# Down-projection terms added to x by VectorE instead of by accumulating DMAs, and a second buffer for the fourth block's parts

## The chip, the core and the metric

The kernel runs on one core of a Trainium2 chip. A core has five engines with a queue each, which run their own instructions in order and wait for one another by semaphores: TensorE (PE in the profile, with its weight loads as PEld), VectorE (DVE), ScalarE (ACT), GpSimd (POOL) and SyncE (SP). TensorE multiplies from the on-chip memory SBUF into eight banks of a second memory, PSUM. VectorE and ScalarE read those banks. DMAs move data between the device memory and SBUF and inside SBUF; those that add to what is at the target are issued by GpSimd here. The metric is the device time of one execution in microseconds (us), lower is better.

## The reference

Two layers of an encoder on 512 tokens of width 1024. Each layer is a gated feed-forward block, a mixer and a second feed-forward block; `x` is the residual stream.

```python
def swiglu(h, w1, w3, w2):
    return (jax.nn.silu(h @ w1) * (h @ w3)) @ w2
...
        h = rmsnorm(x, g_ffn1[l])
        x = x + 0.5 * swiglu(h, w1_a[l], w3_a[l], w2_a[l])
...   # the mixer: p = h @ w_in[l], Fourier, convolution and pooling branches, gates, then
        x = x + merged @ w_o[l]
        h = rmsnorm(x, g_ffn2[l])
        x = x + 0.5 * swiglu(h, w1_b[l], w3_b[l], w2_b[l])
```

`w1` and `w3` are 1024 x 2816, `w2` is 2816 x 1024. There are four feed-forward blocks in all. Everything is float32.

## The kernel before

**Layout.** Activations lie with channels on the 128 partitions and the 512 tokens along the row: `x` is eight tiles `x[0]` to `x[7]` of 128 x 512. Each float32 operand of a matmul is cut into a high part and a low part (what the high part's rounding left), and `mm` (L360) makes three matmuls of one product: high by high, high by low, low by high (L362, L363, L364).

**Jobs of seven products.** Most of the work is done in jobs. A job takes two output blocks of 128 channels and two halves of 256 tokens, thus a 2 x 2 block result, and a number of pairs of input blocks (four pairs for products from `x`, whose operand is called n in the profile; three pairs for the down-projections by `w2`, whose operand is called unit). It needs seven block products M1 to M7 instead of eight. `run` (L559) issues them in the order M1, M5, M4 of the job before, M6, M3 of the job before, M2, M7. They share three PSUM banks: M6, M7 and M4 add into the bank in which M1 began, M3 adds into that of M5, and M2 has one of its own. A result is a sum of banks at certain moments: "11" is M1 and M2; "12" is the first bank after M6 and the M5 bank after M3; "22" is the first bank after M7 and M5; "21" is the first bank after M4.

**How a result leaves.** After M1, M6 and M7, `kept` (L572) has ScalarE copy the first bank into a tile `sM1`, `sM6` or `sM7` (L574), so that the next product can add into the bank. `take` (L705) then has VectorE add the other bank to that copy into the tiles `a` or `b`, 256 tokens at a time (through `tt`, L437); "21" is copied to `a` by ScalarE (L715). When `a` or `b` is whole, a down-projection job adds it to `x[m + 1]` or `x[m]` by a DMA of GpSimd (L716, L718).

**Stages.** In each feed-forward block the input blocks of `w2` come in three phases of six. As soon as a phase's operands are there, four down-projection jobs follow one another (for channels 0 and 1, 2 and 3, and so on). That makes twelve such stages in the program. Between them stand jobs that make gate and up products. The rest of `w2` (input blocks 18 to 21) is done by plain products.

**Weights.** A job's weights are four blocks: the two of the first row come as one load into a raw tile (`first`), the third as z and the fourth as w (`fourth`, w22 in the code). VectorE makes sums and differences of them (L232, L233, L239), ScalarE casts the high parts (L193, L208), and the low parts come in one of two ways: VectorE subtracts (L194), or ScalarE writes the negative (L206) and an accumulating DMA of GpSimd adds the weights from device memory once more (L207). The latter way serves the first row (partl) and the fourth block (part22h and part22l, used by M4 alone). Loads are issued by SyncE (L187).

**What sets the order.** `Layout` (L94) gives each step of each job a due time on a planned clock: the planned time of the product that needs it minus a lead from `AHEAD` (for the fourth block's parts, the step "last", 12 us ahead of M4). `Weights.advance` (L257) goes through the list at each product and makes the steps that are due, in the list's order. A step that finds no free buffer (`BUFS`, L153) stops the list there: what is behind it waits as well. A buffer is given back when the last product that reads it is issued. Tiles of the activations (the units) come from a pool of 51 equal ones (`UNITS`).

Of the kernel before, what the change touches and what calls it, by code (L numbers as in the profile page):

```python
# [13 lines left out]
ALU = mybir.AluOpType  # L14
# [19 lines left out]
UNITS = 51  # L34
# [59 lines left out]
class Layout:  # L94
# [3 lines left out]
             "rest": 8.0, "last": 12.0}  # L98
# [50 lines left out]
class Weights:  # L149
# [3 lines left out]
    BUFS = {"raw": 3, "z": 2, "w22": 2, "part": 6, "part22": 1}  # L153
# [153 lines left out]
def encoder(ctx: ExitStack, tc: tile.TileContext, layout, x_in, w_in, consts_in, gain_in, out):  # L307
# [128 lines left out]
    def tt(out, a, b, op=ALU.mult):  # L436
        nc.vector.tensor_tensor(out=out, in0=a, in1=b, op=op)  # L437
# [92 lines left out]

    def multiply(job, q, ps, start):
        hi, lo = weights.product(job, q)
        k, n = job[2]
        ops = state["g"] if job[0][0][:2] == "w2" else state["n"]
        for j in range(n):
            while k // 2 + j not in ops and ops is not state["n"]:
                one()
            b = ops[k // 2 + j]
            mm(ps, cut((hi, lo), j * P, (j + 1) * P), b[q], start and j == 0, j == n - 1, not start)
# [19 lines left out]
    def run(jobs, take, before=(), after=(), between=None):  # L559
# [12 lines left out]
        def kept(b, q, ps):  # L572
            b["s" + q] = tmp.tile([P, Q], F32, tag="s" + q, name="s" + q, bufs=2)
            nc.scalar.copy(b["s" + q], ps)  # L574

        def product(job, b, q):
# [4 lines left out]
            if q in ("M1", "M6", "M7"):  # L581
                kept(b, q, ps)
# [3 lines left out]
            if q == "M2":  # L586
                late.append(lambda: take(job, "11", ps, b["sM1"], late))
            if q == "M7":
                late.append(lambda: take(job, "22", b["M5"], b["sM7"], late))
            if q == "M4":  # L590
                late.append(lambda: take(job, "21", ps, None, late))
            if q == "M3":
                late.append(lambda: take(job, "12", ps, b["sM6"], late))
# [86 lines left out]
    def ffn(l, s, after, first=False, last=False):  # L680
# [24 lines left out]
        def take(job, which, ps, addend, late):  # L705
            c = slice(0, Q) if which[1] == "1" else slice(Q, S)
# [5 lines left out]
            if job[0][0] == "w2" + s:  # L712
                m = job[0][2] // P
                if which == "21":
                    nc.scalar.copy(a[:, c], ps)  # L715
                    late.append(lambda: nc.gpsimd.dma_start(x[m + 1], a, accum_op=ALU.add))  # L716
                elif which == "12":
                    late.append(lambda: nc.gpsimd.dma_start(x[m], b, accum_op=ALU.add))  # L718
                    if m == KD - 2:
                        state["done"] += 1  # L720
                        made(None)
                return
# [480 lines left out]
```

## Time and profile before

| what | value |
| --- | --- |
| median of 3 runs | 2120.56 us (2116.67 to 2122.01) |
| the profiled execution, its time | 2117.35 us |
| its span, first to last instruction | 2115.4 us |
| mean granted TensorE clock | 0.982 |
| busy share PE, DVE, ACT, POOL | 96%, 70%, 67%, 25% |
| DMA, mean over the span | 181 GB/s |

How to read what follows. A row of a group has the line, the engine, the operation, the tiles written and read (`out<-in`, buffer numbers left out), shapes and count, then the busy time in us and the mean of one in ns, then the engine's idle time just before these instructions and what ended it. A row of the view of waits has the engine, tile and line that waited, what ended the wait, the total in us, the number of waits and the longest. A timeline row has the start in us from the span's start, the duration in us, engine, line, operation and tiles, and in brackets the idle time before it with its releaser. A line may be that of a helper: L437 is every VectorE operation on two tensors. Matmuls overlap in the pipeline, so one lasts longer than the distance to the next.

### The profile page before, as it was taken

How to read it: one execution, taken by the hardware profiler on the slowest of the kernel's cores; microseconds unless marked ns; L12 is line 12 of the kernel's file. 1: busy time of each engine (PE TensorE's matmuls, PEld its weight loads, DVE VectorE, ACT ScalarE, POOL GpSimd, SP SyncE). 2: the span in 40 equal slices, each digit the busy share in tenths (PEclk: the TensorE clock that was granted, in tenths of full speed). 3: DMA queues.
4: the chain of work that ended last, by engine and by line, in shares of the span. 5: the costliest groups of instructions: out<-in, count | busy, mean ns of one | idle time of the engine just before them, and what ended most of it. 6: DMA issues, size and time to landing. Idle time of an engine off the chain costs nothing.

```text
span 2115.4 us, 38561 instructions
## 1 busy us (share of the span) xinstructions
PE 2023.3 (96%) x14886; PEld 1921.1 (91%) x14886; DVE 1487.8 (70%) x2403; ACT 1418.1 (67%) x2442; POOL 537.8 (25%) x628
## 2 busy tenths in 40 slices
PE   8999999899999999999999998998999999999998
PEld 6999998799998899999879998987999988989997
DVE  5867675788875576767667676667798656766864
ACT  7767676776665676767667676667766556767664
POOL 3331322411111423222341322232111123222221
PEclk9999999999999999999999999999999999999999
DMA  8797989767875779797967978887677666797983
GB/s 249 153 217 171 218 176 234 164 139 165 185 179 151 154 157 215 175 215 173 241 145 155 223 173 200 189 219 152 149 179 188 164 168 135 168 220 178 213 193 103
DMA packets 159448, 383.18 MB, mean 181 GB/s; under 512 B 17696, under 2 KB 37536, under 8 KB 159264
## 3 DMA queue, kind: packets, MB, share of 16 engines
q0 software_dynamic: 73008, 175.16, 48.4%
q1 hardware_dynamic: 86112, 205.31, 29.9%
q8 instruction: 116, 1.90, 0.4%
q14 instruction: 68, 0.56, 0.1%
q10 hardware_dynamic: 144, 0.24, 0.0%
HBM read 340.80 MB, written 2.10 MB: 162 GB/s over the span
## 4 chain that ended last, share of the span: by engine, by line
PE 45%; issue 22%; DMA 19%; ACT 5%; POOL 5%; DVE 4%; POOLq 0%; ACTq 0%; DVEq 0%; SPq 0%
PE ps L362 15%; PE ps L364 15%; PE ps L363 15%; DMA part22l<-weights 11%; DMA raw<-weights 3%; DMA w<-weights 3%; DMA n<-t 1%; POOL partl L207 1%; POOL x L716 1%; POOL x L718 1%; ACT parth L208 1%; POOL part22l L207 1%; DVE partl L194 1%; ACT partl L206 1%; POOL b L390 1%
## 5 line engine op out<-in xcount | busy, mean ns | idle before, releaser
L362 PE MATMUL ps<-n,parth 128*128 128x256 f32 x2760 | 780.9, 283 | 15.6 <-ACT sM L574 9.9
L363 PE MATMUL ps<-n,parth 128*128 128x256 f32 x2760 | 780.3, 283 | 11.4 <-DMA n<-t 7.4
L364 PE MATMUL ps<-n,partl 128*128 128x256 f32 x2760 | 778.2, 282 | 0.0
L362 PEld LDWEIGHTS ps<-n,parth 128*128 128x128 f32 x2760 | 523.7, 190 | 19.4 <-ACT sM L574 11.8
L363 PEld LDWEIGHTS ps<-n,parth 128*128 128x128 f32 x2760 | 524.6, 190 | 14.4 <-DMA n<-t 8.5
L364 PEld LDWEIGHTS ps<-n,partl 128*128 128x128 f32 x2760 | 524.1, 190 | 0.0
L207 POOL DMA_DIRECT2D part22l<-weights x163 | 143.4, 879 | 868.5 <-ACT a L725 290.7
L207 POOL DMA_DIRECT2D partl<-weights x200 | 176.0, 880 | 415.7 <-ACT partl L206 190.7
L194 DVE TENSOR_TENSOR partl<-raw,parth 128x1024 fp32r<-128x1024 f32 (+3 forms) x217 | 243.0, 1120 | 43.4 <-ACT parth L193 43.2
L193 ACT CAST parth<-z 128x1024 fp32r<-128x1024 f32 (+1 forms) x163 | 161.0, 988 | 152.7 <-DVE z L233 140.5
L362 PE MATMUL ps<-unit,parth 128*128 128x256 f32 x864 | 248.5, 288 | 2.4 <-ACT sM L574 2.4
L363 PE MATMUL ps<-unit,parth 128*128 128x256 f32 x864 | 247.5, 286 | 0.0
L364 PE MATMUL ps<-unit,partl 128*128 128x256 f32 x864 | 246.7, 286 | 0.0
L574 ACT COPY sM<-ps 128x256 f32<-128x256 f32 x489 | 178.4, 367 | 93.8 <-PE ps L364 92.3
L206 ACT ACTIVATE partl<-raw 128x1024 fp32r<-128x1024 f32 (+2 forms) x200 | 200.4, 1002 | 56.6 <-DMA raw<-weights 38.6
L208 ACT CAST parth<-raw 128x1024 fp32r<-128x1024 f32 (+2 forms) x200 | 197.8, 989 | 56.1 <-PE ps L363 48.3
L232 DVE TENSOR_TENSOR z<-z,w 128x512 f32<-128x512 f32 (+1 forms) x163 | 107.0, 657 | 182.4 <-DMA w<-weights 176.3
L194 DVE TENSOR_TENSOR partl<-z,parth 128x1024 fp32r<-128x1024 f32 (+1 forms) x163 | 186.0, 1141 | 68.2 <-PE ps L364 39.9
L193 ACT CAST parth<-raw 128x1024 fp32r<-128x1024 f32 (+3 forms) x217 | 208.4, 964 | 36.3 <-PE ps L363 30.8
L437 DVE TENSOR_TENSOR b<-ps,sM 128x256 f32<-128x256 f32 x318 | 133.1, 420 | 114.9 <-PE ps L364 113.3
L239 DVE TENSOR_TENSOR raw<-raw,z 128x1024 f32<-128x1024 f32 (+1 forms) x163 | 185.9, 1141 | 18.7 <-ACT partl L206 11.8
L208 ACT CAST part22h<-w 128x512 fp32r<-128x512 f32 (+1 forms) x163 | 95.4, 586 | 133.4 <-PE ps L363 94.7
(191 smaller groups left out, 4130.2 us busy)
## 6 DMA issues: line engine op xcount, KB each, us to landing
raw<-weights SPq DMA_DIRECT2D x187, 512.0 KB, 4.7
partl<-weights POOLq DMA_DIRECT2D x146, 512.0 KB, 6.7
z<-weights SPq DMA_DIRECT2D x115, 256.0 KB, 4.3
w<-weights SPq DMA_DIRECT2D x115, 256.0 KB, 3.7
part22l<-weights POOLq DMA_DIRECT2D x115, 256.0 KB, 4.6
raw<-weights SPq DMA_DIRECT2D x50, 384.0 KB, 4.3
partl<-weights POOLq DMA_DIRECT2D x50, 384.0 KB, 6.4
n<-t POOLq DMA_DIRECT2D x48, 256.0 KB, 4.7
```

The costliest lines, as they stand in the source:

```text
L193: self.nc.scalar.copy(hi[:, :w], src)
L194: self.tail.append((self.t, self.made, lambda: self.nc.vector.tensor_tensor(out=lo[:, :w], in0=src, in1=hi[:, :w].bitcast(F32), op=ALU.sub ...
L206: self.nc.scalar.activation(lo[:, :w], src, AF.Copy, scale=-1.0)
L207: self.nc.gpsimd.dma_start(lo[:, :w], self.source(key), accum_op=ALU.add)
L208: self.nc.scalar.copy(hi[:, :w], src)
L232: v.tensor_tensor(out=z[:, 2 * w : 3 * w], in0=z[:, :w], in1=w22[:, :w], op=ALU.add)
L239: v.tensor_tensor(out=raw, in0=raw, in1=raws.pop(("third", key))[:, : 2 * w], op=ALU.subtract)
L362: nc.tensor.matmul(ps, ah, bh, start=start, stop=False, skip_group_check=more)
L363: nc.tensor.matmul(ps, ah, bl, start=False, stop=False, skip_group_check=more)
L364: nc.tensor.matmul(ps, al, bh, start=False, stop=stop, skip_group_check=more)
L437: nc.vector.tensor_tensor(out=out, in0=a, in1=b, op=op)
L574: nc.scalar.copy(b["s" + q], ps)
```

## The change

For down-projection jobs nothing is kept in sM tiles and nothing goes through `a` and `b`. At each of the seven moments VectorE adds the bank into its quarter of `x` directly (`added`): after M1, M6 and M7 in `kept`, and for "11", "22", "21" and "12" in `take`. The copies of ScalarE, the three adds and the two accumulating DMAs of these jobs are gone; jobs of n are as before. The parts of the fourth block get two buffers, their step is due 13 us ahead of M4, and the pool of units has 50.

```diff
-UNITS = 51
+UNITS = 50
...
-             "rest": 8.0, "last": 12.0}
+             "rest": 8.0, "last": 13.0}
...
-    BUFS = {"raw": 3, "z": 2, "w22": 2, "part": 6, "part22": 1}
+    BUFS = {"raw": 3, "z": 2, "w22": 2, "part": 6, "part22": 2}
...
+    def downwards(job):
+        return job[0][0][:2] == "w2"
+
+    def added(job, which, ps):
+
+        out = x[job[0][2] // P + int(which[0]) - 1][:, int(which[1]) * Q - Q : int(which[1]) * Q]
+        tt(out, ps, out, ALU.add)
...
-        def kept(b, q, ps):
+        def kept(job, b, q, ps):
+            if downwards(job):
+                return added(job, {"M1": "11", "M6": "12", "M7": "22"}[q], ps)
             b["s" + q] = tmp.tile([P, Q], F32, tag="s" + q, name="s" + q, bufs=2)
             nc.scalar.copy(b["s" + q], ps)
...
         def take(job, which, ps, addend, late):
+            if downwards(job):
+                added(job, which, ps)
+                if which == "12" and job[0][2] == D - 2 * P:
+                    state["done"] += 1
+                    made(None)
+                return
...
-            if job[0][0] == "w2" + s:
-                m = job[0][2] // P
-                if which == "21":
-                    nc.scalar.copy(a[:, c], ps)
-                    late.append(lambda: nc.gpsimd.dma_start(x[m + 1], a, accum_op=ALU.add))
-                elif which == "12":
-                    late.append(lambda: nc.gpsimd.dma_start(x[m], b, accum_op=ALU.add))
-                    if m == KD - 2:
-                        state["done"] += 1
-                        made(None)
-                return
```

TensorE's order of matmuls is the same in both but for how two pairs of rows are grouped. Two other queues show what moves.

VectorE, in the first stage, about one job's length in its middle; the tiles x_86 to x_93 are `x[0]` to `x[7]`, L194 makes low parts, L232 and L233 the sums of a later job, L239 its difference. Before:

```order
119 L232 TENSOR_TENSOR z<-z,w_1332 128x384
120 L437 TENSOR_TENSOR b<-ps,sM_1295 128x256
121 L233 TENSOR_TENSOR z<-z,raw 128x384
122 L194 TENSOR_TENSOR partl<-raw,parth 128x768
123 L437 TENSOR_TENSOR a<-ps,sM_1385 128x256
124 L239 TENSOR_TENSOR raw<-raw,z 128x768
125 L194 TENSOR_TENSOR partl<-z,parth 128x768
126 L437 TENSOR_TENSOR b<-ps,sM_1345 128x256
```

And with the change:

```order
120 L437 TENSOR_TENSOR x_88<-ps,x_88 128x256
121 L232 TENSOR_TENSOR z<-z,w_1292 128x384
122 L233 TENSOR_TENSOR z<-z,raw 128x384
123 L437 TENSOR_TENSOR x_87<-ps,x_87 128x256
124 L437 TENSOR_TENSOR x_88<-ps,x_88 128x256
125 L437 TENSOR_TENSOR x_86<-ps,x_86 128x256
126 L239 TENSOR_TENSOR raw<-raw,z 128x768
127 L437 TENSOR_TENSOR x_88<-ps,x_88 128x256
128 L194 TENSOR_TENSOR partl<-raw,parth 128x768
129 L437 TENSOR_TENSOR x_89<-ps,x_89 128x256
130 L194 TENSOR_TENSOR partl<-z,parth 128x768
131 L437 TENSOR_TENSOR x_89<-ps,x_89 128x256
```

Seven adds stand where three stood, spread between the weight steps, and L232 and L233 are now next to each other, for a job further ahead.

GpSimd in the same stage. Before:

```order
29 L207 DMA part22l<-weights 128x384
30 L716 DMA x_87<-a 128x512
31 L718 DMA x_86<-b 128x512
32 L207 DMA partl<-weights 128x1024
33 L207 DMA part22l<-weights 128x384
34 L716 DMA x_89<-a 128x512
35 L718 DMA x_88<-b 128x512
36 L207 DMA partl<-weights 128x1024
```

And with the change:

```order
28 L207 DMA part22l<-weights 128x384
29 L207 DMA partl<-weights 128x768
30 L207 DMA part22l<-weights 128x384
31 L207 DMA partl<-weights 128x768
32 L207 DMA part22l<-weights 128x384
33 L207 DMA partl<-weights 128x1024
34 L207 DMA part22l<-weights 128x512
35 L207 DMA partl<-weights 128x1024
```

Only the weights' DMAs are left, and part22l and partl take turns without a transfer into x between them.

More of the change, by code (lines that the diff above doesn't have):

```diff
@@ L533, in multiply @@
         k, n = job[2]
-        ops = state["g"] if job[0][0][:2] == "w2" else state["n"]
+        ops = state["g"] if downwards(job) else state["n"]
         for j in range(n):
@@ L581, in product @@
             if q in ("M1", "M6", "M7"):
-                kept(b, q, ps)
+                kept(job, b, q, ps)
             flush()
@@ L586, in product @@
             if q == "M2":
-                late.append(lambda: take(job, "11", ps, b["sM1"], late))
+                late.append(lambda: take(job, "11", ps, b.get("sM1"), late))
             if q == "M7":
-                late.append(lambda: take(job, "22", b["M5"], b["sM7"], late))
+                late.append(lambda: take(job, "22", b["M5"], b.get("sM7"), late))
             if q == "M4":
@@ L592, in product @@
             if q == "M3":
-                late.append(lambda: take(job, "12", ps, b["sM6"], late))
+                late.append(lambda: take(job, "12", ps, b.get("sM6"), late))
         def other(pieces, n=2):
```

## The prediction

> **What bounds the kernel now.** I read the view of TensorE's waits first, then the busy time by stretch, then the timeline of one stage.
>
> ```profile
> PE 2023.3 (96%) x14886; PEld 1921.1 (91%) x14886; DVE 1487.8 (70%) x2403; ACT 1418.1 (67%) x2442; POOL 537.8 (25%) x628
> ...
> PE ps L364 <- DMA part22l<-weights: 31.3, 25, 3.7
> PE ps L362 <- ACT sM L574: 18.8, 18, 2.1
> PE ps L362 <- ACT pfh L896: 7.7, 2, 3.9
> PE ps L363 <- DMA n<-t: 7.4, 5, 2.6
> ```
>
> TensorE (PE) sets the time, so an edit that leaves its matmuls alone can only shorten waits. The two largest are for part22l, the low part of a job's fourth weight block, and for sM, the ScalarE copy that frees a bank.
>
> Both gather in the down-projections. There are twelve stages of four down-projection jobs. Below stand the first and the last of the twelve rows of one answer (each stage with the edges that it shares with its neighbours) and their sum, then one stretch between stages and the sum of eight such stretches. The columns are the stretch, its length, busy time (and count) of PE, PEld, DVE, ACT and POOL, granted clock, DMA share, GB/s.
>
> ```profile
> 105.10:148.40 43.30, 39.41 (x316) 38.80 (x315) 28.00 (x44) 27.46 (x51) 13.68 (x16) 0.96 0.94 213
> ...
> 2024.30:2066.80 42.50, 39.57 (x316) 38.76 (x315) 26.22 (x40) 25.86 (x49) 12.21 (x14) 0.96 0.93 208
> sum 510.10, PE 469.54 PEld 461.01 DVE 324.10 ACT 320.13 POOL 155.18; mean PE 39.13 PEld 38.42 DVE 27.01 ACT 26.68 POOL 12.93
> ...
> 1971.90:2024.30 52.40, 52.40 (x446) 52.40 (x445) 40.97 (x67) 39.04 (x68) 11.74 (x15) 1.00 0.80 184
> ...
> sum 428.90, PE 420.71 PEld 419.26 DVE 328.36 ACT 312.28 POOL 92.98; mean PE 52.59 PEld 52.41 DVE 41.05 ACT 39.03 POOL 11.62
> ```
>
> The stretch from 1971.9 runs without a gap: 52.40 us / 446 = 0.1175 us a matmul, at DMA share 0.80 and VectorE (DVE) 78% busy. At that pace the 316 matmuls of a stage take 37.1 us, twelve stages 445.6 us. They take 510.1, so **64.5 us is lost there**, at DMA share 0.92 to 0.97. The other stretches lose 53.6 - 52.4 = 1.2 us each.
>
> The loss has three parts. The groups name the waits:
>
> ```profile
> L364 PE MATMUL ps<-unit,part22l 128*128 128x256 f32 x144 | 46.0, 319 | 31.6 <-DMA part22l<-weights 31.3
> L362 PE MATMUL ps<-unit,part22h 128*128 128x256 f32 x144 | 42.5, 295 | 6.6 <-ACT sM L574 6.6
> L362 PE MATMUL ps<-unit,parth 128*128 128x256 f32 x864 | 248.5, 288 | 2.4 <-ACT sM L574 2.4
> L362 PE MATMUL ps<-n,parth 128*128 128x256 f32 x2760 | 780.9, 283 | 15.6 <-ACT sM L574 9.9 <-ACT half L930 5.7
> ```
>
> All 31.3 us for part22l fall into down-projections ("unit" is their operand, "n" that of the others); of sM 6.6 + 2.4 = 9.0 do, and 9.9 fall into the jobs that follow. The third part is the clock: over the twelve rows, length times what the granted clock lacks to 1.00 adds up to 17.1 us (0.04 of 43.3 and 42.5 in the two shown; three rows lack nothing, one lacks 0.08). 31.3 + 9.0 + 17.1 = 57.4 of 64.5; 7.1 us are short waits.
>
> Why part22l is late shows the timeline of the first stage:
>
> ```profile
> 125.37 0.28 PE L364 MATMUL ps<-unit,part22l 128*128 128x256 f32 x1
> ...
> 126.03 0.52 ACT L206 ACTIVATE part22l<-w 128x384 fp32r<-128x384 f32 x1
> ...
> 126.58 0.33 SPq L187 DMA_DIRECT2D w<-weights  x1
> ...
> 126.95 0.90 POOL L207 DMA_DIRECT2D part22l<-weights  x1 [1.26 <-ACT a L715]
> ...
> 131.99 0.28 PE L363 MATMUL ps<-unit,part22h 128*128 128x256 f32 x1
> 133.21 0.87 POOL L718 DMA_DIRECT2D x<-b  x1 [3.70 <-issue]
> 133.76 0.69 DVE L232 TENSOR_TENSOR z<-z,w 128x512 f32<-128x512 f32 x1 [4.39 <-DMA w<-weights]
> ...
> 135.13 0.58 PE L364 MATMUL ps<-unit,part22l 128*128 128x256 f32 x1 [2.87 <-DMA part22l<-weights]
> 135.51 0.42 PE L362 MATMUL ps<-unit,part22h 128*128 128x256 f32 x1
> ```
>
> With one buffer, ScalarE (ACT) may refill part22l only after the last M4 has read it (125.4); the accumulating DMA goes out at 126.95 and has landed by 135.1, some 8 us on a crowded fabric, while the next M4 wants it at 132.1. The raw block w, freed by the same refill, is loaded only at 126.58, and VectorE stands 4.39 us for it. Behind the wait the matmuls run at 0.42 to 0.58 us in place of 0.28: that is the clock term.
>
> **The change, part by part.** *Removed:* in each of 48 jobs three sM copies, one copy to a, three adds of sM, and two DMAs that add a and b to x.
>
> ```profile
> L574 ACT COPY sM<-ps 128x256 f32<-128x256 f32 x489 | 178.4, 367 | 93.8 <-PE ps L364 92.3
> L437 DVE TENSOR_TENSOR b<-ps,sM 128x256 f32<-128x256 f32 x318 | 133.1, 420 | 114.9 <-PE ps L364 113.3 <-DMA x<-b 0.7
> L437 DVE TENSOR_TENSOR x<-ps,x 128x512 f32<-128x512 f32 x40 | 27.5, 688 | 33.0 <-PE ps L364 32.9
> L716 POOL DMA_DIRECT2D x<-a x48 | 53.2, 1108 | 2.1 <-ACT parth L193 1.3 <-DMA raw<-weights 0.8
> ...
> q0 software_dynamic: 73008, 175.16, 48.4%
> x<-a POOLq DMA_DIRECT2D x48, 256.0 KB, 6.9
> ```
>
> ScalarE loses 4 x 0.37 = 1.5 us a job, 5.9 us of its 26.7 a stage, none of it on the path but where a bank waits. The 96 DMAs are 25.2 MB of the 175.16 MB on q0, whose packets took 48.4% of 2115.4 us: about 147 us of all sixteen engines, 12.3 us a stage (an estimate by the queue's mean). The DMA work of a stage falls from about 0.95 x 42.5 = 40.4 to 28.1 us, 76% of 37.1: less than the 0.80 beside which the gapless stretch ran. GpSimd (POOL) no longer issues these 96 DMAs, nor waits ahead of them (the 3.70 us at 133.21).
>
> *Added:* seven adds into x a job in place of three, at the 0.42 us of the row b<-ps,sM (same shape, one operand in the bank, one in SBUF; x<-ps,x at twice the width, 0.69, agrees). Back to back they cost less, since the next starts before the last has ended:
>
> ```profile
> 96.69 0.42 DVE L437 TENSOR_TENSOR unit<-unit 128x256 f32<-128x256 f32 x1
> 97.02 0.41 DVE L437 TENSOR_TENSOR a<-ps,sM 128x256 f32<-128x256 f32 x1
> ```
>
> So 16 more a stage cost 5.3 to 6.7 us, and VectorE goes from 27.0 to 32.3-33.7 of 37.1 us: 87 to 91%. M6 adds into M1's bank, M7 into M6's and M4 into M7's, each two products of nine matmuls later, 2 x 9 x 0.1175 = 2.1 us. In that time VectorE must now have read the bank. In the order an add stands at worst behind one 0.7-1.0 us operation and another add or two, about 1.8 us with itself; what can break this is L232's wait for w just ahead of adds. I set 0.3 us a stage, 4 us in all, between nothing and the rival below. Units fall from 51 to 50: the last gate product before a stage (L459) now stands among the adds of its second and third job in the order (it waits for a tile, as I read it); what it makes is used a whole stage later, cover enough (0.7 us of VectorE each if not).
>
> *Moved:* two buffers let the step "last" run when the plan says, and what stands behind it in the list too. A buffer was held from 12 us ahead of M4 to M4, while a job's seven products last 7 x 9 x 0.1175 = 7.4 us in these stages; two buffers give 14.8 us for the 13 now planned. The refill, about 0.5 + 0.5 on ScalarE, 0.9 to issue and 8 us to land, fits in 13 at today's landing times, so **part22l: 31.3 to 0**. The load of w leaves earlier as well, and so does L232. That bears on the wait after a stage:
>
> ```profile
> 162.07 0.69 DVE L232 TENSOR_TENSOR z<-z,w 128x512 f32<-128x512 f32 x1 [2.49 <-DMA w<-weights]
> ...
> 164.87 1.05 ACT L193 CAST parth<-z 128x1024 fp32r<-128x1024 f32 x1 [3.30 <-DVE z L233]
> 165.82 0.37 ACT L574 COPY sM<-ps 128x256 f32<-128x256 f32 x1
> ...
> 166.24 0.39 PE L362 MATMUL ps<-n,parth 128*128 128x256 f32 x1 [0.82 <-ACT sM L574]
> ```
>
> w late, so L232 late, the cast behind it, the copy behind the cast, TensorE. Of these 9.9 us I take 8 (0 to 9.9).
>
> *Clock:* the half-speed stretches follow waits of two to three us, and those go. I take 15.4 of 17.1, one of ten remaining.
>
> The page "TensorE: Matmul & The Clock Gate" of the Trainium skill, section "HAM oscillation — how this bites in real kernels", asks for no TensorE idle gap over about 3.4 us. Here 2.87 us was followed by slow matmuls, so the trace does not agree with that bound. By the rule hardly one wait here would count, the slow clock would have another cause and stay, and the sum below would be 15 us later.
>
> **Sum.** 31.3 + (9.0 - 4.0) + 15.4 + 8.0 = 59.7 us. The profiled execution took 2117.35 us (span 2115.4 and 1.95 around it): **2057.7, forecast 2058**. It lies 3.2 us below the median of 2120.56, within the runs shown. If all 64.5 + 9.9 = 74.4 go it is 2043; with none of the 8 us after the stages, four slow stretches left and 1 us more a stage of waits for adds, 2057.7 + 8 + 5.1 + 12 = 2083.
>
> **The rivals.** *VectorE becomes the bound (0.13).* At 87 to 91% in order, each job once finds an add behind a 0.87 us step with its slack used: 48 x 0.87 = 42 us more, **2096**. For it: no stretch shown runs VectorE over 78%. Against: VectorE still stands about 4 us a stage, and ScalarE had 26.7 of 42.5 with the same duty.
>
> "VectorE: DVE Perf Modes" of the Trainium skill, "The DRAIN you can't avoid", says that the next operation does not start until the pipe is empty. The starts above, 0.33 us apart with 0.42 long, disagree; by the rule 91% is the figure and this rival has 0.2.
>
> *The transfers are hidden anyway (0.05).* If weight loads alone keep the fabric full, part22l is as late with two buffers, only the bank waits change: 2117 less some 3 us, **2114**. Against it stands the DMA share of 0.80 between stages, with part22 on one buffer, too, and no wait for it.
>
> *Slower (0.03).* Adds stand behind L232. If in every second job it waits 4.39 us for w as at 133.76, TensorE loses what exceeds the slack, 4.39 - 2.1 = 2.3, and 1.7 us of clock: 24 x 4.0 = 96, less 60, **2153**. It decides from 60 / 48 = 1.2 us a job. Against: w leaves earlier, on an emptier fabric.
>
> **How the numbers follow.** The forecast's case has 0.79, its own range 2043 to 2083. I end at 2044 to 2090: about 0.05 lies below, and above it most of the 0.13 and the two small cases. About 0.3% (6 us) is what a measurement here can tell. Faster: 0.79 + 0.13 = 0.92; same: the hidden case, 0.05; slower 0.03.
>
> **What would show it.** Right: no wait of TensorE for part22l with "unit"; stages of 37.5 to 38.5 us at clock 1.00 and DMA share below 0.8; VectorE near 33 us a stage; L232's waits well below 176 us. Wrong: TensorE's waits at L362 or L363 put down to DVE x in every job (VectorE the bound); part22l waits that stay with the DMA share over 0.9 (hidden); long L232 waits with DVE x behind them (slower).

## The result, and the profile after

The changed kernel took **2034.92 us** (median of 4 runs, 2033.19 to 2037.22) against 2118.61 us (4 runs) for the kernel before: ratio 0.9614, 95% interval 0.9578 to 0.9649. It is faster, as forecast. Yet 2034.92 lies 23 us below the forecast of 2058 and 9 us below the range of 2044 to 2090: the gain was 84 us, and the sum had 59.7. On another chip, where the kernel before took 2128.8, the changed kernel took 2035.65 (6 runs).

The profiled execution took 2033.19 us, its span is 2031.4. The totals by engine, and the view of TensorE's waits, in the columns of the prediction's first fence:

```profile
PE 1989.9 (98%) x14886; PEld 1898.5 (93%) x14886; DVE 1547.5 (76%) x2595; ACT 1364.6 (67%) x2250; POOL 455.5 (22%) x532
```

```profile
PE ps L363 <- DMA n<-t: 9.0, 6, 2.1
PE ps L362 <- ACT pfh L901: 7.1, 2, 3.8
PE ps L362 <- ACT half L935: 5.7, 2, 2.8
PE ps L363 <- DVE n L437: 4.4, 3, 2.5
PE ps L362 <- ACT parth L193: 2.8, 2, 2.5
```

The waits for part22l (31.3 us) and for sM (18.8) are gone from the list. What is left belongs to the mixer and to the making of n. No wait for the new adds has come in: TensorE waits nowhere for VectorE's x.

The busy time by stretch, the first and the last of the twelve stages and their sum, then the sum of the eight stretches between stages that the prediction summed:

```profile
108.40:145.30 36.90, 36.90 (x316) 36.90 (x315) 31.69 (x59) 22.03 (x34) 7.93 (x9) 1.00 0.89 207
...
1946.10:1983.00 36.90, 36.90 (x315) 36.90 (x315) 30.21 (x55) 22.37 (x34) 7.96 (x9) 1.00 0.83 188
sum 443.70, PE 443.70 PEld 443.70 DVE 377.03 ACT 265.82 POOL 94.70; mean PE 36.98 PEld 36.98 DVE 31.42 ACT 22.15 POOL 7.89
...
sum 417.30, PE 417.30 PEld 417.30 DVE 334.13 ACT 314.14 POOL 77.16; mean PE 52.16 PEld 52.16 DVE 41.77 ACT 39.27 POOL 9.64
```

In every one of the twelve stages TensorE is busy for the whole stretch, at clock 1.00. A stage takes 443.7 / 12 = 36.98 us, where before 42.5. It has reached its floor with these matmuls: 316 at 0.117 us, without a gap. The 84.0 us by which the spans differ are 510.1 - 443.7 = 66.4 in the stages, 428.9 - 417.3 = 11.6 in the eight stretches, and 6.0 in the rest of the program.

VectorE is busy for 31.4 of 37.0 us in a stage (85%) and stands in no one's way. The DMA share is 0.88, averaged over the twelve rows by length. So the DMA engines still have 0.88 x 36.98 = 32.4 us of work in a stage; before it was 40.4, and the prediction had 28.1.

The chain of waits, first line by engine, of before and then of after:

```profile
PE 45%; issue 22%; DMA 19%; ACT 5%; POOL 5%; DVE 4%; POOLq 0%; ACTq 0%; DVEq 0%; SPq 0%
```

```profile
PE 87%; DMA 3%; ACT 3%; issue 2%; DVE 2%; POOL 2%; POOLq 0%; SPq 0%; ACTq 0%; DVEq 0%
```

Before, the chain that ended last ran through TensorE for under half of the span; 19% of it were DMAs, and 22% is what the view calls issue, time in which an engine waited for nothing that the profile shows. Now it is TensorE's own work but for an eighth. The groups show VectorE's wait for w, which the prediction named as the cause behind the slower rival (176.3 us before, 27.6 now), and the adds (376 of them at 0.45 us, idle time before them only for TensorE's own results):

```profile
L437 DVE TENSOR_TENSOR x<-ps,x 128x256 f32<-128x256 f32 (+1 forms) x376 | 164.0, 448 | 76.4 <-PE ps L364 76.3
...
L232 DVE TENSOR_TENSOR z<-z,w 128x512 f32<-128x512 f32 (+1 forms) x163 | 108.2, 664 | 41.5 <-DMA w<-weights 27.6 <-DMA z<-weights 13.9
```

### The profile page after: what moved, and what is told of

Its sections match the earlier page's. It is cut to its first block, busy times and chain, and to the rows that moved or that the text cites. A ratio compares the mean times of both kernels' runs of the same rounds, so it can differ in the third digit from the quotient of the medians.

```text
span 2031.4 us, 38426 instructions
## 1 busy us (share of the span) xinstructions
PE 1989.9 (98%) x14886; PEld 1898.5 (93%) x14886; DVE 1547.5 (76%) x2595; ACT 1364.6 (67%) x2250; POOL 455.5 (22%) x532
## 4 chain that ended last, share of the span: by engine, by line
PE 87%; DMA 3%; ACT 3%; issue 2%; DVE 2%; POOL 2%; POOLq 0%; SPq 0%; ACTq 0%; DVEq 0%
PE ps L363 29%; PE ps L362 29%; PE ps L364 29%; DMA n<-t 1%; DMA z<-weights 1%; DMA raw<-weights 1%; ACT parth L208 1%; ACT b L388 1%; POOL b L390 1%; DVE t L476 1%; ACT hh L379 1%; DMA w<-weights 1%; DVE t L437 0%; POOL n L489 0%; ACT partl L206 0%
## 5 line engine op out<-in xcount | busy, mean ns | idle before, releaser
L194 DVE TENSOR_TENSOR partl<-raw,parth 128x1024 fp32r<-128x1024 f32 (+3 forms) x217 | 242.8, 1121 | 40.0 <-ACT parth L193 39.7
L363 PE MATMUL ps<-unit,parth 128*128 128x256 f32 x864 | 242.6, 281 | 0.0
L362 PE MATMUL ps<-unit,parth 128*128 128x256 f32 x864 | 242.6, 281 | 0.0
L364 PE MATMUL ps<-unit,partl 128*128 128x256 f32 x864 | 242.1, 280 | 0.0
L437 DVE TENSOR_TENSOR x<-ps,x 128x256 f32<-128x256 f32 (+1 forms) x376 | 164.0, 448 | 76.4 <-PE ps L364 76.3
L239 DVE TENSOR_TENSOR raw<-raw,z 128x1024 f32<-128x1024 f32 (+1 forms) x163 | 186.2, 1143 | 23.0 <-ACT partl L206 16.3
L194 DVE TENSOR_TENSOR partl<-z,parth 128x1024 fp32r<-128x1024 f32 (+1 forms) x163 | 185.7, 1139 | 1.4 <-ACT parth L193 1.4
L437 DVE TENSOR_TENSOR b<-ps,sM 128x256 f32<-128x256 f32 x222 | 93.1, 420 | 117.2 <-PE ps L364 117.1
L584 ACT COPY sM<-ps 128x256 f32<-128x256 f32 x345 | 126.9, 368 | 77.0 <-PE ps L364 75.1
```

Source lines behind the costliest of these rows:

```text
L194: self.tail.append((self.t, self.made, lambda: self.nc.vector.tensor_tensor(out=lo[:, :w], in0=src, in1=hi[:, :w].bitcast(F32), op=ALU.sub ...
L239: v.tensor_tensor(out=raw, in0=raw, in1=raws.pop(("third", key))[:, : 2 * w], op=ALU.subtract)
L362: nc.tensor.matmul(ps, ah, bh, start=start, stop=False, skip_group_check=more)
L363: nc.tensor.matmul(ps, ah, bl, start=False, stop=False, skip_group_check=more)
L364: nc.tensor.matmul(ps, al, bh, start=False, stop=stop, skip_group_check=more)
```

## The experiments

The prediction put the gain on two things: the second buffer (part22l, the clock, the wait after a stage) and, for a smaller part, the transfers that are gone. The first question was which of the two it was. Where nothing else is said, a stage below is the mean length of the twelve, from the view of busy time by stretch, and ratios are to the kernel before on the same chip. Where kernels of different chips are compared, it is by these ratios: that of the changed kernel itself was 0.9614 on one chip and 0.9579 on another.

### The two halves apart

**The adds alone**: the changed kernel with one buffer, 12 us and 51 units, as before.

```diff
-UNITS = 50
+UNITS = 51
-             "rest": 8.0, "last": 13.0}
+             "rest": 8.0, "last": 12.0}
-    BUFS = {"raw": 3, "z": 2, "w22": 2, "part": 6, "part22": 2}
+    BUFS = {"raw": 3, "z": 2, "w22": 2, "part": 6, "part22": 1}
```

> The adds alone: the changed kernel with one buffer for the fourth block's parts, the step 12 us ahead and 51 units, as before. Theory T (two causes, late refill of the one buffer and a crowded fabric, each making the other worse): the transfers are gone, so a refill takes about 0.5 + 0.5 + 0.9 us and 4.4 us to land, 6.3 us, where the time from the end of one M4 to the first low part of the next is about 6.6 us; it nearly fits, TensorE waits for part22l some 5 to 15 us in all, and the time is 2050 to 2080, say 2065. Rival A (the transfers alone were the cause): 2033 to 2040. Rival B (the one buffer alone was the cause): 2105 to 2120, with the 31 us of part22l waits still there.

**The buffers alone**: the same three lines the other way round, on the kernel before.

> The buffers alone: the kernel before with two buffers for the fourth block's parts, the step 13 us ahead and 50 units; the copies, the a and b tiles and the 96 accumulating DMAs stay. Theory T: the DMA work of a stage is still about 40.4 us against 37.0 us of matmuls, so a stage cannot fall below about 40.4 (from 42.5); with the 10 us after the stages the time is 2075 to 2100, say 2085, and the DMA share in the stages stays over 0.95. Rival B (the buffer alone): 2033 to 2045, part22l waits gone. Rival A (the transfers alone): 2110 to 2120, no gain.

**The transfers alone taken away**: the kernel before without its two DMAs into x. Its x lacks what the stages add.

```diff
-                    late.append(lambda: nc.gpsimd.dma_start(x[m + 1], a, accum_op=ALU.add))
-                    late.append(lambda: nc.gpsimd.dma_start(x[m], b, accum_op=ALU.add))
```

> The transfers alone taken away: the kernel before without the two accumulating DMAs of each down-projection job, so that x lacks the terms of the twelve stages; one buffer, the ScalarE copies and the adds into a and b stay. Theory T: like the adds alone, 2050 to 2080, and what differs from that run is what the ScalarE copies cost against VectorE's adds (within 10 us). Rival A: 2033 to 2045. Rival B: 2105 to 2120.

**Transfers away and two buffers**: both edits on the kernel before; the sM copies, a and b stay, and x lacks the stages' terms again.

> The fourth corner: the kernel before without the two accumulating DMAs of each down-projection job (x lacks the terms of the twelve stages) and with two buffers, the step 13 us ahead, 50 units; ScalarE's copies and VectorE's adds into a and b stay. Theory T2 (after the first runs: the transfers set the pace as long as they are there, whatever the buffers; without them the one buffer is the next limit): 2033 to 2045, as the changed kernel, since nothing is left to wait for. Rival C (adding straight from the bank by VectorE frees banks sooner than ScalarE's copies, and is worth time of its own): 2050 to 2065, with TensorE's waits for sM as without the DMAs.

Measured, with the kernel before at 2121.7 (16 runs) on the chip of the first three and 2121.9 (7 runs) on that of the fourth:

| | one part22 buffer | two, 13 us, 50 units |
| --- | --- | --- |
| transfers into x | 2121.7, stage 42.5 (before) | 2131.54, ratio 1.0049 [1.0029, 1.0070], stage 43.8 |
| no transfers, sM copies stay | 2071.19, 0.9765 [0.9739, 0.9791], stage 39.2 | 2039.95, 0.9598 [0.9561, 0.9635], stage 37.0 |
| adds by VectorE | 2075.06, 0.9784 [0.9758, 0.9810], stage 40.1 | 2034.92, 0.9614 [0.9578, 0.9649], stage 37.0 (after) |

Three things follow. The buffer alone (with its lead of 13 us and the 50 units) gains nothing, it costs 0.5%. The transfers alone are worth 50 us, and only when they are gone is the buffer worth another 1.7%, some 36 us. And that the sums are made by VectorE in place of ScalarE's copies changes little: the last two rows differ by 4 us with one buffer, and their intervals overlap in both columns. The change works by the transfers that it takes away and the buffer that this makes useful, not by what it moves between VectorE and ScalarE.

TensorE's waits with the transfers gone and one buffer (the second of these rows in the table):

```profile
PE ps L362 <- ACT sM L574: 14.7, 27, 1.7
...
PE ps L364 <- DMA part22l<-weights: 6.4, 10, 1.3
```

With one buffer, the part22l waits fall from 31.3 us to 6.4. In the kernel with the adds alone they fall to 1.3. In the kernel with the buffers alone they are gone altogether: its view of waits has no row for part22l, as the prediction had it for two buffers at today's landing times. So either half of the change removes nearly all of this wait. But in the kernel with the buffers alone the time did not go with the wait:

```profile
sum 525.00, PE 472.01 PEld 466.06 DVE 316.81 ACT 325.74 POOL 161.57; mean PE 39.33 PEld 38.84 DVE 26.40 ACT 27.14 POOL 13.46
```

Its stages take 43.8 us, and TensorE is idle in them for 525.00 - 472.01 = 53.0 us. The timeline in the middle of a stage shows for what:

```profile
906.96 0.88 POOL L718 DMA_DIRECT2D x<-b  x1
913.00 0.42 DVE L437 TENSOR_TENSOR b<-ps,sM 128x256 f32<-128x256 f32 x1 [3.38 <-DMA x<-b]
913.34 0.41 DVE L437 TENSOR_TENSOR a<-ps,sM 128x256 f32<-128x256 f32 x1
...
913.81 0.39 PE L362 MATMUL ps<-unit,parth 128*128 128x256 f32 x1 [1.30 <-DVE a L437]
```

The transfer of b into x is issued at 906.96 and has landed 6 us later; VectorE may write a later b into the same buffer only when it has landed, and TensorE stands behind VectorE. The waits of this kind came to 104.3 us on VectorE (25 times, 0.7 us in the kernel before) and 58.0 us on TensorE:

```profile
PE ps L362 <- DVE a L437: 58.0, 29, 4.8
```

The wait changed its place, from the weights to x. Why these transfers now are the ones that come late (other transfers may be in flight beside them), the runs don't tell. Nor does the amount of DMA work explain the length: by length-weighted share, a stage of this kernel has 0.90 x 43.75 = 39.5 us of it, 2.5 us more than its matmuls take, and lasts 6.8 us longer than they do. The time expected from the DMA work alone, 2075 to 2100, was missed.

### Is it load, or GpSimd's queue?

The transfers go through GpSimd's queue, between the DMAs for part22l and partl. They could cost by their place there, or by what they load on the DMA engines. Two kernels put 96 DMAs back into the changed kernel, two a job at the old moments. They add zeros: 256 KB each in the first, 1 KB each in the second.

```diff
+    nothing = const.tile([P, S], F32, name="nothing")
+    nc.vector.memset(nothing, 0.0)
...
+                if which in ("21", "12"):
+                    m = job[0][2] // P + (which == "21")
+                    late.append(lambda: nc.gpsimd.dma_start(x[m], nothing, accum_op=ALU.add))
```

In the second, the last line has `x[m][:, :2], nothing[:, :2]`.

> The transfers alone put back: the changed kernel with two accumulating DMAs of 256 KB per down-projection job that add zeros to x, issued where a and b were added before; two buffers stay. Theory T: DMA work of about 40.4 us against 37.0 us of matmuls in each stage, so at least 12 x 3.4 = 41 us more than the changed kernel, 2070 to 2095, like the buffers alone. Rival B (the second buffer hides the transfers): 2033 to 2045. Rival A: 2105 to 2120.

> The changed kernel with the two accumulating DMAs per down-projection job as in the run with the transfers put back (same waits for VectorE's adds on GpSimd's queue, zeros added to x), but each of 2 columns, 1 KB in place of 256 KB. What is left is the queue: waiting for an add ahead of the weights' DMAs, and 0.9 us to issue. Theory Q (it is GpSimd's order that makes partl late): 2090 to 2115, the waits for partl after each stage stay. Rival F (it is the load on the fabric): 2035 to 2050, the waits for partl are gone.

With the load: 2115.53 us, ratio 0.9970 [0.9948, 0.9993], nearly all of the gain gone. With the short ones: 2038.33 us, 0.9592 [0.9557, 0.9627], nothing lost, though GpSimd issues as many DMAs. So it is what the transfers carry, not that they are issued. Whether the bytes count by their place in this queue or by their load on all sixteen engines is not shown, since no run moved them by another queue. The first of the two, by its waits, then one of them in the timeline:

```profile
PE ps L366 <- DMA partl<-weights: 57.6, 13, 5.6
```

```profile
133.67 0.90 POOL L207 DMA_DIRECT2D partl<-weights  x1 [1.22 <-ACT part22l L206]
...
141.86 0.57 PE L366 MATMUL ps<-n,partl 128*128 128x256 f32 x1 [4.91 <-DMA partl<-weights]
```

and the busy time by stretch, first stage and sum:

```profile
106.20:149.80 43.60, 38.69 (x316) 38.49 (x315) 32.00 (x59) 21.98 (x34) 13.99 (x16) 0.96 0.96 216
...
sum 523.90, PE 468.03 PEld 465.57 DVE 379.66 ACT 265.57 POOL 166.13; mean PE 39.00 PEld 38.80 DVE 31.64 ACT 22.13 POOL 13.84
```

A stage has 0.946 x 43.66 = 41.3 us of DMA work again (by length-weighted share), more than the 37.0 us that its matmuls take. In all three kernels with the transfers a stage has 39.5 to 41.3 us of it and takes 42.5 to 43.8, and which wait takes up the difference depends on the kernel: part22l before, a and b with two buffers, partl here. Here it comes once in a stage and late, as I read it because two buffers let the loads run ahead; it costs as much. The time of 2115.53 is above the 2070 to 2095 expected from the DMA work: the stages last 2.1 to 4.3 us longer than that work in these three kernels. The half clock behind the waits is part of this; that the work sets the length is argued, not shown.

### What the second buffer frees

With the transfers gone, the second buffer is worth 1.7% (0.9784 to 0.9614), yet TensorE hardly waits for part22l there (1.3 us). It waits for VectorE's adds. The waits of the adds alone, then VectorE, SyncE and ScalarE in its second stage:

```profile
PE ps L362 <- DVE x L437: 22.5, 23, 2.1
```

```profile
223.23 0.42 DVE L437 TENSOR_TENSOR x<-ps,x 128x256 f32<-128x256 f32 x1 [0.49 <-PE ps L364]
225.76 0.69 DVE L232 TENSOR_TENSOR z<-z,w 128x512 f32<-128x512 f32 x1 [2.10 <-DMA w<-weights]
226.37 0.95 DVE L194 TENSOR_TENSOR partl<-raw,parth 128x768 fp32r<-128x768 f32 x1
227.24 1.08 DVE L437 TENSOR_TENSOR x<-ps,x 128x256 f32<-128x256 f32 x3
...
220.41 0.52 ACT L206 ACTIVATE part22l<-w 128x384 fp32r<-128x384 f32 x1
...
220.95 0.33 SPq L187 DMA_DIRECT2D w<-weights  x1
...
227.80 0.36 PE L362 MATMUL ps<-unit,part22h 128*128 128x256 f32 x1 [1.42 <-DVE x L437]
```

ScalarE reads the raw block w at 220.41, in the refill of part22; the next w is loaded into its place at 220.95 and is there at 225.7. L232 waits 2.10 us for it, L194 and three adds come behind, and TensorE waits 1.42 us for the first of these. That is the chain of the prediction's slower rival, in this kernel and not in the changed one. With one buffer the refill waits for M4, so w is held till then, and besides the list of steps stops at the refill. Three kernels take these apart, all with one part22 buffer.

**The list goes on**: a blocked step "last" is passed over for up to five steps behind it.

```diff
-            while self.splits and self.splits[0][0] <= t and self.step(*self.splits[0][1:]):
-                self.splits.pop(0)
+            while self.one_step(t):
...
+    def one_step(self, t):
+        for i, s in enumerate(self.splits[:6]):
+            if s[0] > t:
+                break
+            if self.step(*s[1:]):
+                self.splits.pop(i)
+                return True
+            if s[1] != "last":
+                break
+        return False
```

> The adds alone (one buffer, 12 us, 51 units), but a step "last" that finds no buffer no longer stops the list: the up to five steps behind it that are due go ahead. By the plan's own times sums and differences in the stages get back the leads that two buffers give them (8.6 and 7.5 us in place of 5.7 and 3.2), while "last" itself and the load of w stay as late as with one buffer (6.8 us, 15.0 us). Theory L (what the second buffer gave, once the transfers were gone, was that the list no longer stood still): 2033 to 2050. Rival W (it was the refill itself and the raw block w that it holds): 2060 to 2080, as the adds alone (2075), with VectorE still waiting some 120 us for w at L232.

**The list goes on, and a third raw w**, and **a third raw w alone** (the list stops):

```diff
-    BUFS = {"raw": 3, "z": 2, "w22": 2, "part": 6, "part22": 1}
+    BUFS = {"raw": 3, "z": 2, "w22": 3, "part": 6, "part22": 1}
```

> The adds alone with one part22 buffer and a list that goes on past a blocked last step, and now three raw tiles w in place of two (units 51). It asks what a second part22 buffer frees. Theory R (the raw block w: it stays held until part22 is free, so the next w is loaded late, L232 waits for it and the adds into x stand behind L232): a third w takes its place, L232's waits for w fall from 105 us to under 50, TensorE's waits for DVE x from 11.4 to under 3, the mean stage from 39.5 to 37.0-37.6 us, the time from 2070 to 2036-2046. Theory P (the refill itself: the parts come late because their one buffer is free late): TensorE's waits for part22l stay at 6-10 us, the stage at 39 or more, the time at 2062-2074.

> The adds alone with one part22 buffer, the list stopping at a blocked last step as in before, and three raw tiles w. Theory R (raw block w held): as with the list that goes on, 2036-2050, since loads of w aren't held by the list. If the stopped list matters beside w: the steps sums behind last still come late, L232 waits for nothing but starts late, TensorE waits for DVE x or for parth, 2060-2075. Theory P (refill itself): 2062-2076 too, but with waits for part22l of 6 us or more.

| one part22 buffer, adds by VectorE | two raw w | three raw w |
| --- | --- | --- |
| list stops | 2075.06, 0.9784 [0.9758, 0.9810], stage 40.1 | 2052.80, 0.9651 [0.9610, 0.9691], stage 38.4 |
| list goes on | 2070.10, 0.9730 [0.9685, 0.9774], stage 39.5 | 2037.40, 0.9581 [0.9548, 0.9613], stage 37.2 |

The four were on three chips (before at 2121.7, 2125.5 and 2128.8), so the ratios are what to compare. One part22 buffer with a third w and a list that goes on is as fast as the changed kernel on the same chip (2035.65, 0.9579 [0.9550, 0.9607]). In it TensorE's wait for part22l is 0.2 us: the parts themselves need no second buffer once the transfers are gone. A third w is worth 1.3 to 1.5%. The list is worth 0.7% with a third w, measured on one chip; with two it is 0.5%, but on two chips and with intervals that overlap, too little to be sure of. Together they are the second buffer's worth (1.7 to 2.0%). The third w alone, at 2052.80, lies between the two cases that were expected of it: w and the list both count. The sum of the stages and L232's wait, with both:

```profile
sum 445.80, PE 445.31 PEld 444.47 DVE 381.51 ACT 268.50 POOL 94.46; mean PE 37.11 PEld 37.04 DVE 31.79 ACT 22.37 POOL 7.87
```

```profile
DVE z L232 <- DMA w<-weights: 15.6, 8, 10.8
```

That wait is 119.6 us with the adds alone, 105.4 when the list goes on, 15.9 with a third w alone, 15.6 here.

### Is VectorE near its bound?

The prediction gave 0.13 to VectorE as the bound. Two kernels add one, and two, more reads of the bank to each of a job's four "11", "22", "21" and "12", thus 4 and 8 more VectorE operations a job, into a tile that no one reads.

```diff
+    spare, spare2 = (const.tile([P, Q], F32, name=f"spare{k}") for k in range(2))
+    nc.vector.memset(spare2, 0.0)
...
+                for _ in range(1):
+                    tt(spare, ps, spare2, ALU.add)
```

> The changed kernel with 4 more VectorE operations of 128x256 per down-projection job, each reading the bank that the add before it read, so that they can run nowhere else (in the runs before the extra operations had no such tie and were made far ahead of their place). VectorE was busy 31.4 us of the 37.0 of a stage; 16 more at 0.33 to 0.42 us make it 36.7 to 38.1. Theory T2 (VectorE's slack in a stage is some 5.5 us): stages of 37.0 to 38.5 us, the time 2035 to 2055. Rival (the queue's order makes TensorE wait long before VectorE is full): 2060 to 2100.

> The same with 8 more per job: VectorE 42.0 to 44.8 us a stage. Theory T2: VectorE is the bound, stages of 42 to 45 us, 12 x 5 to 8 us more and some clock: 2095 to 2145. Rival (made up between the stages, where VectorE is 78% busy): 2050 to 2085.

With 4: 2036.50 us, 0.9579 [0.9543, 0.9616], VectorE 33.4 of 36.96 us in a stage (90%), and still no wait of TensorE in the stages:

```profile
sum 443.50, PE 443.50 PEld 443.50 DVE 400.90 ACT 252.00 POOL 94.69; mean PE 36.96 PEld 36.96 DVE 33.41 ACT 21.00 POOL 7.89
```

The 36.7 to 38.1 us expected of VectorE did not come: 16 operations were added to a stage, but only 10 to 12 more stand in it (69 in place of 59 in the first), so others have moved out of it, and the step is smaller than it was meant to be.

With 8: 2113.81 us, 0.9947 [0.9919, 0.9976]. But this kernel's order of jobs around the stages is another (346 matmuls lie in a stage's stretch in place of 316, and TensorE waits 33.9 us for partl), so it is no larger dose of the same thing and says nothing on VectorE's bound.

Two earlier ones made the same numbers of operations from SBUF alone (`tt(spare, spare2, spare2, ALU.add)`).

> The changed kernel with 4 more VectorE operations of 128x256 per down-projection job that nothing needs. At 0.33 to 0.42 us each a stage gets 5.3 to 6.7 us more, so VectorE is busy 37.0 to 38.4 us of the 37.0 us that the matmuls take. Theory T2 (VectorE has some 5 us a stage to spare and no more): 2035 to 2065, first waits of TensorE for VectorE's adds. Rival (an operation in the queue costs its time, slack or not): 2035 + 12 x 5.3 to 6.7 = 2099 to 2115.

> The changed kernel with 8 more such VectorE operations per job: 42.3 to 45.1 us of VectorE a stage against 37.0 us of matmuls. Theory T2 (then VectorE is the bound): stages of 42 to 46 us, the time 2095 to 2145. Rival (VectorE's work runs far enough ahead to be made up between the stages, where it is 78% busy): 2060 to 2090.

They miss their aim: tied to nothing, the operations were all put into the first 376 and 699 us. 2051.18 us (0.9653 [0.9617, 0.9689]) and 2056.39 us (0.9679 [0.9636, 0.9721]); the 16 to 21 us above the changed kernel arose mostly outside the stages. The first three stages of the second show something all the same:

```profile
111.80:148.70 36.90, 36.90 (x316) 36.90 (x315) 36.32 (x74) 21.95 (x34) 7.92 (x9) 1.00 0.90 206
202.50:240.50 38.00, 37.53 (x316) 37.05 (x315) 37.72 (x76) 22.31 (x34) 8.33 (x10) 1.00 0.90 204
292.80:329.70 36.90, 36.90 (x316) 36.90 (x315) 36.60 (x73) 22.39 (x34) 7.92 (x9) 1.00 0.91 209
```

VectorE is busy for 98 to 99% of these stages, and two of the three are at the floor, the other 1 us above it.

### The largest wait that is left

After the change TensorE's largest wait is 9.0 us for n<-t: accumulating DMAs that make the low parts of two of four pairs of n. In this kernel VectorE makes all four by subtraction, as it did two, and the 48 DMAs are gone.

```diff
-        for i in (3, 0):
+        for i in (3, 1, 0, 2):
             nc.scalar.copy(pairs[i][0], sources[i])
-        for i in (1, 2):
-            nc.scalar.activation(pairs[i][1], sources[i], AF.Copy, scale=-1.0)
-            nc.gpsimd.dma_start(pairs[i][1], sources[i], accum_op=ALU.add)
-        for i in (1, 2):
-            nc.scalar.copy(pairs[i][0], sources[i])
-        for i in (3, 0):
+        for i in (3, 1, 0, 2):
             tt(pairs[i][1], sources[i], pairs[i][0].bitcast(F32), ALU.subtract)
```

> The changed kernel with the same exchange at another place: the low parts of all four operand pairs that are made from x (tile n from t, 48 accumulating DMAs of 256 KB in all) by VectorE's subtraction after the high part's cast, in place of ScalarE's negative and a DMA. The changed kernel waits 9.0 us for these DMAs and 4.4 us for VectorE there. If the exchange carries over: the 9 us go and a few us of half clock behind them, 2022 to 2032. If VectorE is what is late at that place: 48 x 0.69 us more of it, its waits grow by what the DMA's shrink, 2033 to 2050.

This gave 2033.41 us, 0.9562 [0.9526, 0.9598], on another chip than the changed kernel's runs, too close to tell. Both were then run on one chip:

> The changed kernel with the low parts of the operand pairs n made by VectorE subtractions, without the copies and 48 accumulating DMAs that made two of four so. In it the 9.0 us for which TensorE waits for n<-t should go; if nothing takes their place it is 5 to 9 us faster than the changed kernel on the same chip (2026-2031 where that has 2035). If VectorE's subtractions come as late as the DMAs did, its waits for DVE n grow by as much and it is within 3 us of it.

> The changed kernel itself, beside the others on one chip: 2033-2037, ratio 0.958-0.963.

2031.36 us (6 runs, 2028.43 to 2035.90; 0.9553 [0.9526, 0.9580]) against 2035.65 us (6 runs, 2033.99 to 2044.06; 0.9579 [0.9550, 0.9607]). The medians differ by 4.3 us, 0.2%; the intervals of the ratios overlap, since both carry the spread of the kernel before, but five of the six times are below the lowest of the changed kernel. It is probably some 4 us faster than the changed kernel, and so than both. Its waits:

```profile
PE ps L362 <- ACT pfh L896: 7.2, 2, 3.8
PE ps L362 <- ACT half L930: 5.5, 2, 2.8
PE ps L363 <- DVE n L437: 4.9, 4, 1.4
PE ps L364 <- DVE pfl L897: 3.6, 2, 1.9
```

The 9.0 us for n<-t are gone, 3.6 us for pfl have come, the rest is nearly as it was.

## Why the prediction was wrong, step by step

**What bounds the kernel: right.** The loss lay in the twelve stages, 64.5 us above the pace of 0.1175 us a matmul, and 66.4 went there.

**The sum took too little of what it had found.** The forecast was 24.3 us too high against its own execution (59.7 predicted, 84.0 in the spans). By terms:

| term of the prediction | predicted | measured | missing |
| --- | --- | --- | --- |
| part22l | 31.3 | 31.3 | 0 |
| sM in the stages less new waits for adds | 9.0 - 4.0 | 9.0 - 0 | 4.0 |
| clock in the stages | 15.4 | 17.1 | 1.7 |
| the "short waits" of the stages | not in the sum | 7.1 | 7.1 |
| stages below the pace of 0.1175 us | not in the sum | 1.9 | 1.9 |
| outside the stages | 8.0 | 17.6 | 9.6 |

This is the step that put the time outside the range: the sum. It charged 4.0 us for new waits that did not come, and it left out gains that did.

*The "short waits".* The prediction wrote "7.1 us are short waits" and never asked what became of them. They weren't waits: TensorE is idle in the stages for 510.10 - 469.54 = 40.6 us, and the two named waits are 40.3 of that. The 7.1 lie in its busy time. Most of it is a hidden part of the same waits: idle time is counted from the end of a matmul, which lasts 0.28 us, while the next would start 0.117 us behind its start, so each wait costs 0.16 us more than its row says. For the 34 waits in the stages (25 for part22l, 9 of the 18 for sM) that is some 5.5 us, an estimate.

*Outside the stages.* The sum took 8.0 of sM's 9.9 us and nothing else. The loss of "1.2 us each" in the eight stretches is mostly that same wait: TensorE is idle there for 428.90 - 420.71 = 8.2 us, all of it for sM. The stretches gained 11.6, so 3.4 more in TensorE's busy time. The rest of the program gained 6.0; 1.7 of that are two more waits for sM, and where the other 4.3 come from is open (the runs of the kernel before alone span 13.8 us). The bound "If all 64.5 + 9.9 = 74.4 go it is 2043" had none of this and was thus no lower bound, and the range stood on it.

**"Two buffers ... part22l: 31.3 to 0": the wait went, but the buffer alone would not have gained the time.** This is the mechanism that failed. The prediction took the single buffer for the cause and the crowded DMA engines for a circumstance ("8 us on a crowded fabric"), and so the wait's 31.3 us for the buffer's worth. The runs show that the wait is not the cost: two buffers with the transfers remove it too, and the kernel is 0.5% slower, with 58.0 us of waits behind VectorE's a in its place. Without the transfers and with one buffer it is 0.2 to 8.5 us in five kernels. That the sum's 31.3 came true all the same is in part luck: the change had both halves. What the buffer does give, once the transfers are gone, is an earlier w and a list that goes on. The prediction had both links ("The load of w leaves earlier as well, and so does L232"), but put them under the 8 us after a stage. They are worth 1.7 to 2.0%, some 36 to 43 us.

**"The DMA work of a stage falls from 40.4 to 28.1": mis-sized.** It fell to 32.4, by 8.0 and not by 12.3. The queue's mean was too high a price for a transfer within SBUF; this was called an estimate there. Nothing hung on it, since 32.4 is still below 37.0. The sign it named, a DMA share under 0.8, was wrong: at 0.88 nothing waits.

**The adds: right in place, too dear.** The 4.0 us of new waits did not come. VectorE's work grew by (377.03 - 324.10) / 12 = 4.4 us a stage, below the 5.3 to 6.7 given, to 85% where 87 to 91 was said.

**The clock: right, and more.** The prediction set its 15.4 us against the page "TensorE: Matmul & The Clock Gate" of the Trainium skill, section "HAM oscillation — how this bites in real kernels", whose bound of about 3.4 us of idle would have left the slow clock in place. All 17.1 us went with the waits, so for these stages the trace decides against the bound. In the kernel with the adds alone, the only two stages with a clock under 1.00 are those with single waits of 2.1 and 1.8 us, while the stage between them has a wait of 1.55; in the kernel without transfers no wait of a stage is over 1.3 us, and no stage is slowed:

```profile
1796.90:1839.20 42.30, 39.44 (x315) 38.72 (x314) 31.47 (x58) 22.37 (x33) 7.69 (x9) 0.96 0.76 179
1891.60:1930.60 39.00, 37.45 (x316) 37.18 (x315) 30.10 (x56) 21.35 (x32) 7.16 (x9) 1.00 0.81 196
1983.00:2024.70 41.70, 39.43 (x316) 38.71 (x315) 31.03 (x56) 23.13 (x34) 7.67 (x9) 0.96 0.73 172
```

But the traces give no other threshold in its place. In the kernel before, a stage whose longest wait was 1.68 us was slowed, and one with a wait of 2.06 us was not:

```profile
1178.76 0.39 PE L364 MATMUL ps<-unit,part22l 128*128 128x256 f32 x1 [1.68 <-DMA part22l<-weights]
1958.67 0.38 PE L364 MATMUL ps<-unit,part22l 128*128 128x256 f32 x1 [2.06 <-DMA part22l<-weights]
```

```profile
1150.30:1192.00 41.70, 39.51 (x316) 38.71 (x315) 27.63 (x44) 27.00 (x51) 13.30 (x16) 0.96 0.96 217
1930.20:1971.90 41.70, 38.04 (x315) 37.22 (x315) 27.30 (x44) 26.50 (x51) 13.06 (x16) 1.00 0.96 216
```

What holds in every run is that no stage was slowed without a wait of at least 1 us ahead of the slow stretch.

**The rivals.** VectorE as the bound fell: 85% without a wait, 90% without a wait in the kernel with four more reads of the bank. So the rule of "The DRAIN you can't avoid", the section of "VectorE: DVE Perf Modes" in the Trainium skill by which this rival would have had 0.2 in place of 0.13, did not bite here. The section itself adds that an operation which is not held starts earlier, which the prediction left out; the starts in the prediction's own fence, 0.33 us apart with 0.42 long, fit that. The hidden transfers fell: at 0.88 the share is still high, and no part22l wait is left. The slower case fell in the changed kernel, but its chain is most of what the adds alone lose against it; the prediction's reason against it ("w leaves earlier") is the second buffer.

## What to carry to other kernels

Compare the DMA work of a stage (share times length) with its matmul time before asking which wait to remove: where it was larger here, removing a wait moved it to the next transfer, and only less traffic helped; where it was smaller, buffers decided. When a buffer is doubled, ask what else its owner held back, here a raw tile and the steps behind it in a list, since that may be worth more than the wait that carries its name. And where a cause is removed from a stage, the sum must say of every part of the loss what becomes of it, the small ones and those just outside too.

## What was not expected of the hardware

A DMA share of 0.88 (0.91 with the 96 short DMAs in the queue) cost TensorE nothing in the stages, while in the three kernels with more DMA work than a stage has matmul time the share stood at 0.90 to 0.95 and a stage took 42.5 to 43.8 us in place of 37.0. The 25.2 MB of transfers into x took about 8 us of all sixteen engines a stage off (40.4 to 32.4), and 8.9 on when put back with zeros (41.3). VectorE at 98% of a stage held up TensorE by 1 us at most. And a stretch of half clock followed a single wait of 1.7 us in one stage (and two of 1.3 and 1.1 us within 4 us in one of the kernel whose list goes on), while waits of 2.1 us in the kernel before and of 3.3 us in the one with eight more reads of the bank were not followed by any: the length of a wait alone does not tell.
